# ConvGLU of a hybrid decoder layer: gate, up and down products in 2x2 blocks, seven block products in place of eight

## The chip, the cores and the metric

The kernel runs on one core of one Trainium2 chip. The metric is the device time of one execution in microseconds (us), the median of several runs. TensorE (PE) multiplies, VectorE (DVE), ScalarE (ACT) and GpSimd (POOL) do the elementwise work, SyncE (SP) issues the transfers between DRAM and SBUF, PEld is the loading of TensorE's weights.

## What is computed

One decoder layer on 2048 tokens of 1024 channels in float32: mixers (sliding-window attention and RWKV-7 side by side, not touched here), the output projection with its residual, the ConvGLU and a final norm.

```python
x = x + concatenate([att, rw], axis=-1) @ w_out
h = rms_norm(x, norm2_g)
u = h @ w_gate                                   # (2048,1024) @ (1024,2816)
c = conv_b + sum(conv_w[j] * pad(u)[:, j:j + T] for j in range(3))
x = x + (silu(c) * (h @ w_up)) @ w_down          # (2048,2816) @ (2816,1024)
return rms_norm(x, final_g)
```

## The kernel before

**Precision.** Every operand of the large products is split in a high part (a copy rounded to the matmul type, made on ACT) and a low part (the value minus the high part, on DVE or POOL). `mm3` (L189; through the helper `mm` all matmuls carry L104) adds three matmuls for each 128 rows of the contraction: high x high, high x low, low x high. Each is 128x128 weights against 512 columns.

**Phase A**, until about 1299 us, is the mixers. Its instructions follow an order that is written out by hand. From `order["on"] = False` on (L1236) the Tile framework's scheduler sets the order in which each engine's queue is filled; the queues themselves run in order.

**Output projection, second part.** `o_job` (L1295) makes 128 tokens x 512 output channels with 24 matmuls from the mixers' output (`catT` in DRAM), adds the residual and leaves the row `x2` in `acc` or in DRAM (`x2d`). `half_prep` (L1312) norms four such rows, transposes them (L1328), scales them on ACT and keeps the transposed, split `h` of a half of the tokens (1024) in SBUF: `hh`, `hl`.

**Gate and up.** For each half `hf` and each of 22 tiles `f` of 128 features, `gate_up(f)` loads 512 KB of each weight, splits it (`split_w`, L1269; low part on POOL, L1276) and for two quarters `q` of 512 tokens runs 24 matmuls into `pg` and 24 into `pu`. ACT and DVE apply the convolution over tokens (`cc`; `halo` carries the last two tokens), the silu and the product; `ah` and `al` (POOL, L1385) are the split result, which stays in SBUF.

**Down.** After each two feature tiles `down` (L1388) adds their product with w_down to the rows `acc`: for 8 token tiles and 2 column halves 6 matmuls into `pd` and one addition on DVE. `gate_up` runs one group ahead of `down`. After the last group each row of the half is squared on ACT (`jo`), scaled on DVE with `rso` and `fgb` (the final norm's weights) and written.

The second half's `half_prep` stands between the last `gate_up` and the last two `down` of the first half, so there TensorE always has down matmuls in its queue. PSUM's eight banks are two pools of four: `ps_gu` and `ps_dn`.

Of the kernel before, what the change touches and what calls it, by code (L numbers as in the profile page):

```python
# [83 lines left out]
def hybrid_trunk_kernel(  # L84
# [1152 lines left out]
    # ================= output projection, second part, and ConvGLU =================  # L1237
    with ExitStack() as B:
        h2 = B.enter_context(tc.tile_pool(name="h2", bufs=1))
        sp = B.enter_context(tc.tile_pool(name="fsp", bufs=2))  # L1240
# [13 lines left out]
        fgb = bc.tile([P, D], F32, name="fgb")  # L1254

        def ffn_consts():
# [6 lines left out]
            nc.sync.dma_start(out=fgb, in_=final_g.rearrange("(o d) -> o d", o=1).broadcast_to([P, D]))

        halo = bc.tile([P, NF, 2], F32, name="halo")
        wg3 = ffn_w_gate[0].rearrange("(k p) f -> p k f", p=P)
        wu3 = ffn_w_up[0].rearrange("(k p) f -> p k f", p=P)

        def split_w(src, tag, name, bufs, pool=gp, lpool=None):  # L1269
            s = wp.tile([P, D], F32, tag="st", name=f"s_{name}", bufs=3)  # L1270
            sv = s.rearrange("p (k f) -> p k f", k=NK) if len(src.shape) == 3 else s
            nc.sync.dma_start(out=sv, in_=src)
            a = pool.tile([P, D], F32R, tag=tag + "h", name=f"h_{name}", bufs=bufs)
            l = (lpool or pool).tile([P, D], F32R, tag=tag + "l", name=f"l_{name}", bufs=bufs)
            act(a, s, AF.Copy)
            (tt if tag == "cat" else nc.gpsimd.tensor_tensor)(out=l, in0=s, in1=f32(a), op=ALU.subtract)  # L1276
            return a, l
# [177 lines left out]
```

## Time and profile before

| | |
|---|---|
| median of 3 runs | 2877.03 us (2875.14 to 2879.46) |
| profiled execution, span of its instructions | 2880.8 us |
| TensorE busy | 2814.0 us, 98% |
| DVE, ACT, POOL busy | 49%, 38%, 34% |
| DRAM read, written | 177.35 MB, 27.39 MB |

The span is one execution under the profiler, from its first to its last instruction; it lies 3.8 us above the median of the runs. A busy engine is one with an instruction in it; matmuls overlap each other, so a matmul's own length (390 ns) is more than the distance from one to the next. "Idle before" and "releaser" say what ended an engine's wait.

### The profile page before, as it was taken

Reading aid. Unit: us, or ns where it says so; the run is one execution under the profiler, and the core shown is the slowest. Engines: PE = TensorE matmul, PEld = TensorE weight load, DVE = VectorE, ACT = ScalarE, POOL = GpSimd, SP = SyncE. Lnnn points to the kernel's source line nnn. Section 1 sums busy time; section 2 is a strip of 40 time slices with the busy share of each in tenths; the row PEclk is TensorE's granted clock in tenths of the full one; section 3 lists DMA queues with packets and bytes.
Section 4 is the critical chain, followed back from the end, with each engine's and each line's share of the span. In section 5 each row is a group of like instructions: output and inputs, shape, how many; then the busy total and the mean of one; then the engine's idle time right before and its main releaser. Section 6 shows DMA issues by size and latency. Waiting matters only on the chain.

```text
span 2880.8 us, 41403 instructions
## 1 busy us (share of the span) xinstructions
PE 2814.0 (98%) x16003; PEld 2196.6 (76%) x16003; DVE 1404.7 (49%) x3223; ACT 1108.6 (38%) x2430; POOL 985.1 (34%) x893
## 2 busy tenths in 40 slices
PE   7899999999999999999999999999999999999998
PEld 5567777777767677768788888888888888888887
DVE  5567666766776667435323333333372333333335
ACT  4356555655565556443322222222242222212222
POOL 6334443443434334321143322233333333322232
PEclk8899999999999999999999999999999999999999
DMA  4222222222232222346521111111133111111111
GB/s 123 61 65 66 71 70 67 63 70 71 64 91 61 61 61 73 94 129 198 186 64 47 51 52 45 44 50 53 59 111 109 48 55 47 49 52 44 44 52 59
DMA packets 319159, 207.44 MB, mean 72 GB/s; under 512 B 96704, under 2 KB 285266, under 8 KB 318962
## 3 DMA queue, kind: packets, MB, share of 16 engines
q1 hardware_dynamic: 318354, 204.26, 24.3%
q8 instruction: 126, 2.06, 0.3%
q14 instruction: 71, 0.58, 0.1%
q10 hardware_dynamic: 608, 0.53, 0.1%
HBM read 177.35 MB, written 27.39 MB: 71 GB/s over the span
## 4 chain that ended last, share of the span: by engine, by line
PE 84%; DVE 8%; DMA 4%; ACT 2%; issue 1%; POOL 0%; SPq 0%; ACTq 0%; DVEq 0%; POOLq 0%
PE pg L104 17%; PE pu L104 17%; PE pd L104 16%; PE pc L104 5%; PE po L104 3%; PE pin_r L104 3%; PE pin_k L104 3%; PE pin_q L104 2%; PE poa L104 2%; DVE M L124 2%; PE px L104 2%; DVE Mt L124 2%; PE pS L104 2%; DMA LL<-dL 1%; PE pO L104 1%; PE pin_v L104 1%
## 5 line engine op out<-in xcount | busy, mean ns | idle before, releaser
L124 DVE TENSOR_TENSOR acc<-pd,acc 128x512 f32<-128x512 f32 x352 | 242.6, 691 | 270.1 <-PE pd L104 269.8
L124 DVE SCALAR_TENSOR_TENSOR cc<-pg,fcst,cc 128x511 f32<-128x511 f32 (+1 forms) x176 | 131.9, 749 | 458.9 <-ACT cc L110 455.8
L1385 POOL TENSOR_TENSOR al<-cc,ah 128x512 fp32r<-128x512 f32 x88 | 113.6, 1291 | 477.9 <-ACT ah L110 477.9
L104 PE MATMUL pg<-h2h,l_g 128*128 128x512 f32 x704 | 277.0, 393 | 0.0
L104 PE MATMUL pu<-h2h,l_u 128*128 128x512 f32 x704 | 276.7, 393 | 0.0
L104 PE MATMUL pg<-h2h,h_g 128*128 128x512 f32 x704 | 276.0, 392 | 0.0
L104 PE MATMUL pu<-h2h,h_u 128*128 128x512 f32 x704 | 275.6, 392 | 0.0
L104 PE MATMUL pg<-h2l,h_g 128*128 128x512 f32 x704 | 275.3, 391 | 0.0
L104 PE MATMUL pd<-h_d,ah 128*128 128x512 f32 x704 | 275.1, 391 | 0.0
L104 PE MATMUL pd<-l_d,ah 128*128 128x512 f32 x704 | 275.0, 391 | 0.0
L104 PE MATMUL pd<-h_d,al 128*128 128x512 f32 x704 | 274.7, 390 | 0.0
L104 PE MATMUL pu<-h2l,h_u 128*128 128x512 f32 x704 | 274.6, 390 | 0.0
L110 ACT ACTIVATE cc<-pg,fcst 128x512 f32<-128x512 f32 x88 | 67.8, 770 | 319.6 <-PE pg L104 319.6
L1276 POOL TENSOR_TENSOR l_g<-s_g,h_g 128x1024 fp32r<-128x1024 f32 x44 | 106.2, 2414 | 197.0 <-ACT h_g L110 197.0
L124 DVE TENSOR_TENSOR Mt<-M,LL 128x60 f32<-128x60 f32 (+24 forms) x496 | 154.3, 311 | 35.6 <-DMA LL<-dL 27.0
L1276 POOL TENSOR_TENSOR l_d<-s_d,h_d 128x1024 fp32r<-128x1024 f32 x44 | 105.6, 2401 | 189.6 <-ACT h_d L110 189.6
L124 DVE TENSOR_TENSOR M<-M,Mt 128x60 f32<-128x60 f32 (+24 forms) x496 | 163.7, 330 | 10.9
L124 DVE TENSOR_TENSOR cc<-pu,cc 128x512 f32<-128x512 f32 x88 | 60.9, 692 | 206.4 <-PE pu L104 201.3
L104 PEld LDWEIGHTS pg<-h2l,h_g 128*128 128x128 f32 x704 | 132.2, 188 | 30.2
L104 PEld LDWEIGHTS pu<-h2l,h_u 128*128 128x128 f32 x704 | 132.2, 188 | 30.1
L104 PEld LDWEIGHTS pg<-h2h,l_g 128*128 128x128 f32 x704 | 132.3, 188 | 29.1
L104 PEld LDWEIGHTS pu<-h2h,l_u 128*128 128x128 f32 x704 | 132.3, 188 | 28.8
(324 smaller groups left out, 6407.4 us busy)
## 6 DMA issues: line engine op xcount, KB each, us to landing
s_g<-in_ffn_w_gate_dram SPq DMA_DIRECT2D x44, 512.0 KB
s_u<-in_ffn_w_up_dram SPq DMA_DIRECT2D x44, 512.0 KB
s_d<-in_ffn_w_down_dram SPq DMA_DIRECT2D x44, 512.0 KB
s_cat<-catT SPq DMA_DIRECT2D x20, 512.0 KB
x<-in_x_dram SPq DMA_DIRECT2D x16, 512.0 KB
w_k<-in_w_in_dram SPq DMA_DIRECT2D x16, 512.0 KB
w_r<-in_w_in_dram SPq DMA_DIRECT2D x16, 512.0 KB
w_v<-in_w_in_dram SPq DMA_DIRECT2D x16, 512.0 KB
```

The costliest lines, as they stand in the source:

```text
L104: in_order("pe", nc.tensor.matmul(**kw))
L110: in_order("act", nc.scalar.activation(*args, **kw))
L124: in_order("dve", f(*args, **kw))
L1276: (tt if tag == "cat" else nc.gpsimd.tensor_tensor)(out=l, in0=s, in1=f32(a), op=ALU.subtract)
L1385: nc.gpsimd.tensor_tensor(out=al[:, qs], in0=cc, in1=f32(ah[:, qs]), op=ALU.subtract)
```

## The change

The Strassen-Winograd scheme multiplies two matrices cut in 2x2 blocks with seven block products in place of eight; the blocks are added and subtracted before and after. It is applied twice.

**Gate and up.** A quad is two feature tiles x two quarters of 512 tokens x the contraction in two halves of 4 x 128 rows. It is 7 products of 12 matmuls. `quad_units` makes the seven block sums of the weights on DVE and splits each in `uh` (ACT) and `ul` (POOL, `gsub`, L1255), in a ring of six units. The seven block sums of `h` are made once for each half (`h2_first`, `h2_second`, `h2_third`: 28 splits of 128x512, high on ACT, low on POOL). `quad` runs the products in the order 1, 6, 7, 5, 2, 4, 3; products 2, 4 and 3 are added in the banks of 1, 7 and 5; `take` evacuates. The convolution works on 1024 tokens at a time. For half 1 the 16 raw tiles of `h` are parked in DRAM (`h1raw`) and read when half 0's gate and up are done.

**Down** comes after all of gate and up, for both halves at once: 7 products of 11 steps of 24 matmuls over all eight banks. The seven block sums of the activations are made on DVE (`sa`) when a pair of feature tiles is done and written to DRAM (`actc`), 256 KB for each sum, pair and half; each step of down reads 512 KB of them back and splits them on ACT and POOL. The 22 tiles of w_down (`wd`, 512 KB each) and `fgb` are loaded into memory that gate and up have used; products 1 and 2 load their weights apart (`sb`). The residual rows are read again (`xr`, 32 x 256 KB) and added on POOL after products 2 and 4. The last product's rows are finished after its evacuation.

The pools of the output projection lie over other tiles of phase A than before, and the constants' transpose (`pfc`) is called before the first `o_job`.

```diff
-        ps_gu = B.enter_context(tc.tile_pool(name="ps_gu", bufs=4, space=PSUM))
-        ps_dn = B.enter_context(tc.tile_pool(name="ps_dn", bufs=4, space=PSUM))
+        ps_b = B.enter_context(tc.tile_pool(name="ps_b", bufs=8, space=PSUM, reuse_waits="tile"))
...
+        def h2_split(hf, p, kk, src):
...
+            act(hi, src, AF.Copy)
+            gsub(lo, src, f32(hi))
+            H2[hf, p, kk] = (hi, lo)
...
+        def h2_second(hf, kk, b11, b12, b22):
+            t3 = hp2.tile([P, 512], F32, tag="ht", name=f"t3_{hf}_{kk}", bufs=3)
+            tt(out=t3, in0=b22, in1=b12, op=ALU.subtract)
+            h2_split(hf, 7, kk, t3)
...
+        def quad_units(w3, pr, name):
+            st = quad_load(w3, pr, name)
+            a11, a21 = st[0][:, :, 0:P], st[0][:, :, P:2 * P]
+            a12, a22 = st[1][:, :, 0:P], st[1][:, :, P:2 * P]
+            yield unit(a11, f"{name}_1", shape=4)
+            s3 = up_.tile([P, 512], F32, tag="s3", name=f"s3_{name}", bufs=2).rearrange("p (k f) -> p k f", k=4)
+            vsub(s3, a11, a21)
+            vadd(a21, a21, a22)
+            vsub(a11, a21, a11)
+            yield unit(a11, f"{name}_6", shape=4)
+            yield unit(s3, f"{name}_7", shape=4)
+            yield unit(a21, f"{name}_5", shape=4)
+            vsub(a11, a12, a11)
+            yield unit(a12, f"{name}_2", shape=4)
+            yield unit(a22, f"{name}_4", shape=4)
+            yield unit(a11, f"{name}_3", shape=4)
...
+                if p == 1:
+                    u2 = gp.tile([P, 512], F32, tag="u2", name=f"u2_{name}", bufs=2)
+                    act(u2, ps[1], AF.Copy)
+                elif p == 6:
+                    vadd(u2, ps[6], u2)
+                elif p == 7:
+                    u3 = gp.tile([P, 512], F32, tag="u3", name=f"u3_{name}", bufs=1)
+                    vadd(u3, ps[7], u2)
+                elif p == 5:
+                    take(22, ps[5], u3)
...
+                    act(cc, gr[i][:, 2:], AF.Identity, scale=cw[:, 2, f:f + 1], bias=cb[:, f:f + 1])
+                    stt(out=cc, in0=gr[i][:, 1:HALF + 1], scalar=cw[:, 1, f:f + 1], in1=cc, op0=ALU.mult, op1=ALU.add)
+                    stt(out=cc, in0=gr[i][:, 0:HALF], scalar=cw[:, 0, f:f + 1], in1=cc, op0=ALU.mult, op1=ALU.add)
+                    act(cc, cc, AF.Silu)
...
+                        tmp = gp.tile([P, 512], F32, tag="ct", name=f"ct_{name}_{what}", bufs=2)
+                        vadd(tmp, ps, u)
+                        nc.gpsimd.tensor_tensor(out=cc, in0=tmp, in1=cc, op=ALU.mult)
...
+                vadd(sa[0], c0[:, t2], c1[:, t2])
+                vsub(sa[1], sa[0], c0[:, t1])
+                vsub(c0[:, t2], c0[:, t1], c0[:, t2])
+                vsub(sa[2], c1[:, t1], sa[1])
+                put(5, sa[0])
...
+        wd = [dp.tile([P, D], F32, name=f"wd_{f}") for f in range(NF)]
+        for f in range(NF):
+            nc.sync.dma_start(out=wd[f], in_=ffn_w_down[0, f * P:(f + 1) * P, :])
...
+        for p in ORDER:
+            if p in (1, 6, 7, 5):
+                banks = [bank(f"d{p}_{m}") for m in range(8)]
+            for k in range(NPR):
+                ahead(NU_)
+                ah0, ah1, bu = ready.pop(0), ready.pop(0), ready.pop(0)
+                for m in range(8):
+                    a = (ah0, ah1)[m // 4]
+                    ms_ = slice((m % 4) * P, (m % 4 + 1) * P)
+                    mm3(banks[m], [(a[0][:, ms_], a[1][:, ms_], bu[0], bu[1])],
+                        first=k == 0 and p in (1, 6, 7, 5), last=k == NPR - 1, skip_group_check=p in (2, 4, 3))
+            for m in range(8):
...
+                elif p == 5:
+                    vadd(u3[m], banks[m], u3[m])
+                    square(u3[m], 1, m, 1)
+                    finish(1, m, c21[m], u3[m])
+                else:
+                    vadd(u2[m], banks[m], u2[m])
+                    square(u2[m], 0, m, 1)
+                    finish(0, m, c11[m], u2[m])
```

Three places in the order of the queues. In the rows the numbers at the end of a name are buffer numbers.

POOL's queue between the halves, before (`l_g`, `l_u`: splits of a whole weight tile; `al`: of activations; `ms_f`, `rs_f`: the norm's factors, one number for each row):

```order
L1276 TENSOR_TENSOR l_u_21_19586<-s_u_21_19583,h_u_21_19585 128x1024
L1385 TENSOR_TENSOR al_20_19454<-cc_20_1_19566,ah_20_19453 128x512
L1385 TENSOR_TENSOR al_21_19590<-cc_21_0_19641,ah_21_19589 128x512
L1276 TENSOR_TENSOR l_g_0_20308<-s_g_0_20305,h_g_0_20307 128x1024
L132 TENSOR_SCALAR ms_f_19732<-ms_f_19732 128x1
L132 TENSOR_TENSOR rs_f_19734<-ms_f_19732,mhalf 128x1
L132 TENSOR_SCALAR ms_f_19741<-ms_f_19741 128x1
L132 TENSOR_TENSOR rs_f_19743<-ms_f_19741,mhalf 128x1
```

and now (`h2l_p_kk`: low parts of block sum p of h; `ul`: of weights):

```order
L1255 TENSOR_TENSOR ul_g_0_1_19126<-s_g_0_0_19121,uh_g_0_1_19125 128x512
L1255 TENSOR_TENSOR h2l_7_0_19269<-t_1_0_19266,h2h_7_0_19268 128x512
L1255 TENSOR_TENSOR h2l_7_1_19289<-t_1_1_19286,h2h_7_1_19288 128x512
L1255 TENSOR_TENSOR h2l_7_2_19309<-t_1_2_19306,h2h_7_2_19308 128x512
L1255 TENSOR_TENSOR h2l_5_0_19279<-hr_0_1_19262,h2h_5_0_19278 128x512
L1255 TENSOR_TENSOR h2l_5_1_19299<-hr_1_1_19282,h2h_5_1_19298 128x512
L1255 TENSOR_TENSOR h2l_5_2_19319<-hr_2_1_19302,h2h_5_2_19318 128x512
L1255 TENSOR_TENSOR ul_g_0_6_19149<-s_g_0_0_19121,uh_g_0_6_19148 128x512
L1570 TENSOR_TENSOR cc_21_19055<-ct_u_10_22_19165,cc_21_19055 128x512
L1255 TENSOR_TENSOR ul_g_0_7_19169<-s_g_0_19144,uh_g_0_7_19168 128x512
```

Where small rows stood, 28 splits of h stand among the splits of the next quads' weights.

SP's queue at the end of gate and up: before, the loads of a group's weights stand one after the other to the end:

```order
L1272 DMA s_g_21_24400<-in_ffn_w_gate_dram 128x8x128
L1272 DMA s_u_21_24406<-in_ffn_w_up_dram 128x8x128
L1272 DMA s_d_18_24535<-in_ffn_w_down_dram 128x1024
L1272 DMA s_d_19_24541<-in_ffn_w_down_dram 128x1024
L1272 DMA s_d_20_24675<-in_ffn_w_down_dram 128x1024
L1272 DMA s_d_21_24681<-in_ffn_w_down_dram 128x1024
```

Now (`sa_k`, `sb_k`: activations and weights of step k of product 1, counted from 0):

```order
L1466 DMA sb_3_22925<-in_ffn_w_down_dram 128x512
L1577 DMA actc_10_15831<-sa_1_10_22707 128x512
L1577 DMA actc_10_15809<-sa_1_10_22708 128x512
L1577 DMA actc_10_15820<-cc_20_22565 128x512
L1577 DMA actc_10_15864<-sa_1_10_22709 128x512
L1611 DMA fgb<-in_final_g_dram 128x1024
L1614 DMA wd_22729<-in_ffn_w_down_dram 128x1024
L1614 DMA wd_22730<-in_ffn_w_down_dram 128x1024
...
L1614 DMA wd_22750<-in_ffn_w_down_dram 128x1024
L1466 DMA sb_4_22965<-in_ffn_w_down_dram 128x512
L1461 DMA sa_5_22995<-actc_5_15793 128x1024
```

The last sums of the activations are written, then come `fgb` and all 22 tiles of w_down, then the fifth step's weights.

DVE's queue at the end of the program, before (`acc<-pd`: additions, the others the final scaling):

```order
L124 TENSOR_TENSOR acc_6_20295<-pd_20_6_0_24783,acc_6_20295 128x512
L124 TENSOR_TENSOR acc_6_20295<-pd_20_6_1_24791,acc_6_20295 128x512
L124 TENSOR_TENSOR acc_7_20296<-pd_20_7_0_24799,acc_7_20296 128x512
L124 SCALAR_TENSOR_TENSOR acc_5_20294<-acc_5_20294,rso_24880,fgb 128x512 x2
L124 TENSOR_TENSOR acc_7_20296<-pd_20_7_1_24807,acc_7_20296 128x512
L124 SCALAR_TENSOR_TENSOR acc_6_20295<-acc_6_20295,rso_24892,fgb 128x512 x2
L124 SCALAR_TENSOR_TENSOR acc_7_20296<-acc_7_20296,rso_24904,fgb 128x512 x2
```

and now (`cu`: evacuations of the last product's banks `d`; `c_`: the rows' other half):

```order
L1429 TENSOR_TENSOR cu_3_22784<-d_3_25188,cu_3_22784 128x512
L1429 TENSOR_TENSOR cu_4_22785<-d_4_25189,cu_4_22785 128x512
L124 SCALAR_TENSOR_TENSOR c_0_22773<-c_0_22773,rso_26108,fgb 128x512
L124 SCALAR_TENSOR_TENSOR cu_0_22781<-cu_0_22781,rso_26108,fgb 128x512
L1429 TENSOR_TENSOR cu_5_22786<-d_5_25190,cu_5_22786 128x512
L124 SCALAR_TENSOR_TENSOR c_1_22774<-c_1_22774,rso_26118,fgb 128x512
L124 SCALAR_TENSOR_TENSOR cu_1_22782<-cu_1_22782,rso_26118,fgb 128x512
L1429 TENSOR_TENSOR cu_6_22787<-d_6_25191,cu_6_22787 128x512
L1429 TENSOR_TENSOR cu_7_22788<-d_7_25192,cu_7_22788 128x512
L124 SCALAR_TENSOR_TENSOR c_2_22775<-c_2_22775,rso_26128,fgb 128x512
```

Before, a row is complete every 2.7 us or so of matmuls and is scaled between them; now all eight rows of the last product are complete within its last step, and 16 scalings follow their 8 evacuations.

## Rows read from the trace of the kernel before

**Rows 1.** The page, its first two parts: span; TensorE's busy time, the engines; the span in 40 slices for PE, the granted clock and the DMA.

```profile
span 2880.8 us, 41403 instructions
PE 2814.0 (98%) x16003; PEld 2196.6 (76%) x16003; DVE 1404.7 (49%) x3223; ACT 1108.6 (38%) x2430; POOL 985.1 (34%) x893
PE   7899999999999999999999999999999999999998
PEclk8899999999999999999999999999999999999999
DMA  4222222222232222346521111111133111111111
```

**Rows 2.** The page's chain of the work that ended last: shares of the span by engine, and by line.

```profile
PE 84%; DVE 8%; DMA 4%; ACT 2%; issue 1%; POOL 0%; SPq 0%; ACTq 0%; DVEq 0%; POOLq 0%
PE pg L104 17%; PE pu L104 17%; PE pd L104 16%; PE pc L104 5%; PE po L104 3%; PE pin_r L104 3%; PE pin_k L104 3%; PE pin_q L104 2%; PE poa L104 2%; DVE M L124 2%; PE px L104 2%; DVE Mt L124 2%; PE pS L104 2%; DMA LL<-dL 1%; PE pO L104 1%; P
```

**Rows 3.** The same chain in order of time, in gate and up of half 0: start, length, what.

```profile
1603.57 5.49 PE pg L104 x24
1609.06 5.49 PE pu L104 x24
```

**Rows 4.** Groups of instructions from 1285 us on, three of the nine groups of ConvGLU's matmuls: count, busy time and mean ns of one, idle time before them.

```profile
L104 PE MATMUL pg<-h2h,l_g 128*128 128x512 f32 x704 | 277.0, 393 | 0.0
L104 PE MATMUL pu<-h2h,h_u 128*128 128x512 f32 x704 | 275.6, 392 | 0.0
L104 PE MATMUL pd<-h_d,ah 128*128 128x512 f32 x704 | 275.1, 391 | 0.0
```

**Rows 5.** Stretches of the span: length, then busy time (and instructions) of PE, PEld, DVE, ACT, POOL, granted clock, DMA share, GB/s. Before the output projection's second part, in it, in gate/up/down of half 0 and half 1, and the end.

```profile
1285.00:1300.00 15.00, 13.31 (x57) 10.36 (x57) 9.26 (x12) 5.07 (x8) 4.33 (x3) 1.00 0.79 247
1320.00:1416.00 96.00, 93.22 (x435) 76.71 (x434) 46.47 (x59) 34.97 (x48) 9.39 (x11) 0.98 0.63 197
1500.00:2000.00 500.00, 500.00 (x2189) 410.69 (x2188) 165.85 (x277) 109.24 (x166) 147.57 (x75) 1.00 0.16 49
2300.00:2800.00 500.00, 500.00 (x2188) 410.72 (x2187) 165.71 (x277) 109.69 (x152) 153.29 (x78) 1.00 0.17 50
2860.00:2881.00 21.00, 12.86 (x57) 10.33 (x55) 15.74 (x24) 7.52 (x22) 7.45 (x13) 0.88 0.47 176
```

**Rows 6.** Timeline of PE in the mixers' last gap: the first po matmul and the last one before the mixers go on.

```profile
1282.71 0.50 PE L104 MATMUL po<-woh,h_cat 128*128 128x512 f32 x1 [0.39 <-ACT woh L110]
1289.90 0.40 PE L104 MATMUL po<-woh,h_cat 128*128 128x512 f32 x1
```

**Rows 7.** Timeline in half 0: issue of one 512 KB load, and the copy that waited for it.

```profile
1464.29 0.34 SPq L1272 DMA_DIRECT2D s_d<-in_ffn_w_down_dram  x1
1467.96 1.06 ACT L110 ACTIVATE h_d<-s_d 128x1024 fp32r<-128x1024 f32 x1 [0.74 <-DMA s_d<-in_ffn_w_down_dram]
```

**Rows 8.** Groups of instructions from 1285 us on, on POOL, DVE and ACT: busy time, mean ns of one, idle time before.

```profile
L1385 POOL TENSOR_TENSOR al<-cc,ah 128x512 fp32r<-128x512 f32 x88 | 113.6, 1291 | 477.9 <-ACT ah L110 477.9
L110 ACT ACTIVATE cc<-pg,fcst 128x512 f32<-128x512 f32 x88 | 67.8, 770 | 319.6 <-PE pg L104 319.6
L124 DVE TENSOR_TENSOR l_cat<-s_cat,h_cat 128x1024 fp32r<-128x1024 f32 x19 | 23.3, 1224 | 5.5 <-ACT h_cat L110 5.4
L124 DVE SCALAR_TENSOR_TENSOR acc<-acc,rso,fgb 128x512 f32<-128x512 f32 x32 | 22.4, 745 | 2.6 <-POOL rso L132 2.6
L110 ACT ACTIVATE h2h<-pt,fcst 128x512 fp32r<-128x512 f32 x32 | 20.0, 683 | 21.8 <-PE pt L1328 21.6
L132 POOL TENSOR_TENSOR rs_f<-ms_f,mhalf 128x1 f32<-128x1 f32 x16 | 9.8, 614 | 1.2
L1323 DVE TENSOR_SCALAR xn<-acc,rs_f 128x1024 f32<-128x1024 f32 x8 | 6.0, 753 | 5.2 <-POOL rs_f L132 5.1
L132 POOL TENSOR_SCALAR ms_f<-ms_f 128x1 f32<-128x1 f32 x16 | 6.0, 375 | 75.5 <-ACT xn L110 55.8 <-ACT sq L110 19.7
```

**Rows 9.** Three tiles and DVE's instructions on them: count, then shortest, median and longest in ns, first and last start. hl is a split in the mixers, wol one in the output projection.

```profile
L124 DVE TENSOR_TENSOR hl<-hr,hh x24: 683/693/1770, 262.3 to 1149.0; 128x512 fp32r<-128x512 f32 x24
L124 DVE TENSOR_TENSOR wol<-swo,woh x16: 677/685/1775, 1283.3 to 1396.2; 128x512 fp32r<-128x512 f32 x16
L124 DVE TENSOR_TENSOR acc<-pd,acc x352: 674/692/693, 1484.7 to 2873.5; 128x512 f32<-128x512 f32 x176
```

**Rows 10.** Stretches as in rows 5 where the transfers are dense: in the output projection, and where half 1's rows are read.

```profile
1308.00:1312.00 4.00, 4.00 (x20) 3.30 (x19) 2.35 (x4) 1.39 (x3) 0.81 (x2) 1.00 1.02 349
1312.00:1316.00 4.00, 4.00 (x19) 3.34 (x18) 2.61 (x3) 1.86 (x3) 0.79 (x2) 1.00 1.08 370
2122.00:2126.00 4.00, 4.00 (x19) 3.33 (x18) 2.49 (x4) 2.30 (x4) 1.76 (x4) 1.00 0.91 357
```

**Rows 11.** Timeline of PE where matmuls of 512 columns follow the mixers' small ones.

```profile
1272.82 0.31 PE L104 MATMUL pO<-ptl,vth 128*64 128x128 f32 x1
1274.00 0.63 PE L104 MATMUL poa<-hh,wl_c 128*128 128x512 f32 x1
1274.42 0.63 PE L104 MATMUL poa<-hh,wh_c 128*128 128x512 f32 x1
```

**Rows 12.** Timeline at the end: the last matmul and the last scaling (two).

```profile
2872.47 0.39 PE L104 MATMUL pd<-h_d,al 128*128 128x512 f32 x1
2876.34 1.41 DVE L124 SCALAR_TENSOR_TENSOR acc<-acc,rso,fgb 128x512 f32<-128x512 f32 x2 [0.85 <-POOL rso L132]
```

More of the change, by code (lines that the diff above doesn't have):

```diff
@@ L1259, in ffn_consts @@
             nc.sync.dma_start(out=frow[8 + NF:], in_=conv_w[0].rearrange("i (j p) -> (i j) p", p=P))
-            ps = ps_gu.tile([P, 512], F32, tag="gu", name="pfc")[:, :8 + 4 * NF]
+            ps = bank("pfc")[:, :8 + 4 * NF]
             nc.tensor.transpose(out=ps, in_=frow, identity=ident[:8 + 4 * NF, :8 + 4 * NF])
             nc.vector.tensor_copy(out=fcst, in_=ps)
[L1263 to L1277, printed above, removed]
         def wo_half(e):
@@ new lines, in product, with quad @@
+        def product(ps, u, hf, p, first, last):
+            mm3(ps, [(u[0][:, kk * P:(kk + 1) * P], u[1][:, kk * P:(kk + 1) * P], *H2[hf, p, kk]) for kk in range(4)],
+                first=first, last=last, skip_group_check=not first)
+        def quad(hf, name, take):
+            ps = {}
+            for p in PRODS:
+                ahead(NU_)
+                u = ready.pop(0)
+                if p in (1, 6, 7, 5):
+                    ps[p] = bank(f"q{p}_{name}")
+                    product(ps[p], u, hf, p, True, True)
+                else:
+                    b = {2: 1, 4: 7, 3: 5}[p]
+                    product(ps[b], u, hf, p, False, True)
+                if p == 1:
[8 more added lines that the diff above has]
+                    take(22, ps[5], u3)
+                elif p == 2:
+                    take(11, ps[1], None)
+                elif p == 4:
+                    take(21, ps[7], u2)
+                else:
+                    take(12, ps[5], u2)
@@ new lines, in hybrid_trunk_kernel, with all_units, ahead @@
+        ORDER = (1, 2, 6, 7, 4, 5, 3)
+        steps = [(p, k) for p in ORDER for k in range(NPR)]
+        jobs = [(hf, pr, g) for hf in range(NHALF) for pr in range(NPR) for g in (True, False)]
+        ready = []
+        def all_units():
+            for hf, pr, g in jobs:
+                yield from quad_units(wg3 if g else wu3, pr, f"{'g' if g else 'u'}{hf}_{pr}")
+            for p, k in steps:
+                yield from down_units(p, k)
+        source = all_units()
+        def ahead(n):
+            while len(ready) < n:
+                u = next(source, None)
+                if u is None:
+                    return
+                ready.append(u)
@@ new lines, in finish @@
+        def finish(j, m, ca, cb_):
+            i = tok[j][m]
+            ms = MS[i]
+            rs = sp_.tile([P, 1], F32, tag="rso", name=f"rso_{i}", bufs=4)
+            gts(out=rs, in0=ms[0], scalar1=ms[1], scalar2=RMS_EPS, op0=ALU.add, op1=ALU.add)
+            gtt(out=rs, in0=rs, in1=mhalf[:, 0:1], op=ALU.pow)
+            for e, c in enumerate((ca, cb_)):
+                es = slice(512 * e, 512 * e + 512)
+                stt(out=c, in0=c, scalar=rs, in1=fgb[:, es], op0=ALU.mult, op1=ALU.mult)
+                nc.sync.dma_start(out=out_t[i][:, es], in_=c)
```

358 lines of the change are left out of this document (236 added, 122 removed).

## The prediction, as it was made

> **What bounds the kernel now.** I read the page first. TensorE is busy for 98% of the span at the full granted clock, the other engines for half of it or less, and the DMA for a fifth or less outside one peak [rows 1]. The chain of the work that ended last is TensorE for 84%, and its largest entries are ConvGLU's products pg, pu and pd [rows 2]. In ConvGLU the chain runs through whole groups of 24 matmuls with no other engine between them, 5.49 us a group, so 5.49 / 24 = 0.2288 us a matmul [rows 3]. The nine groups of these matmuls, 704 each, have one length [rows 4]: 9 x 704 = 6336. By stage, TensorE has no idle time in the middle of either half; 2.78 us of it lie in the output projection's stage, 1.69 just before, 8.14 in the last 21 us [rows 5]. So before, a matmul more or less in ConvGLU is 0.2288 us, and nothing else there has a price. The question is whether this stays so when the other engines get more work.
>
> **What it removes.** The changed order has 3696 matmuls for gate/up and 1848 for down, of the same shape (128x128 against 512 columns): 5544, so 792 fewer. 792 x 0.2288 = **181.2 us** less, if TensorE is as seldom idle. What follows are the stalls.
>
> **(a) Output projection and start of gate/up: 18 us.** Before, pieces of the output projection fill the mixers' last gap, 1282.7 to 1290.1: 20 matmuls, 4.6 us [rows 6]. Now its tiles lie over tiles that the last poa reads, so it starts after it: +4.6. The transpose pfc now stands ahead of the first po; its three small loads are queued on SP behind the last x2d write. A 512 KB load takes 3.67 us from issue to use [rows 7]; I take 4 (0 to 6). The weights of the second half of po's contraction come later too: 3. Transposes stand right behind the fourth, eighth and last po group and need the normed rows: after adding and squaring, ms_f 0.375, rs_f 0.614, the scaling 0.753 [rows 8], partly under 24 matmuls of the next group: 3 in all. Gate/up starts after eight copies of 0.683 and one POOL split of 1.291 [rows 8], 6.8 less the transposes meanwhile: 6.5. Sum 21.1, less the 2.8 us of the old stage's own idle time: 18 (bounds 5 and 30).
>
> **(b) Steady gate/up: 12 us.** One pair of feature tiles is 168 matmuls, 38.4 us. In it POOL has 14 splits of 128x512 and 3 products, 17 x 1.291 = 21.9 [rows 8], and 4 small copies: 23.1 (at 0.3 us each, an estimate). DVE has 12 sums of 128x512 from SBUF at 0.69, 4 scalar_tensor_tensor of 128x1024 at about 1.28 (an estimate between 1.224 for that width and 2 x 0.745, [rows 8]) and 11 evacuations from PSUM at 0.69: 21. Each alone fits, at 60% and 55%. But the rows of the same operation show two lengths: hl takes 693 ns in the median and 1770 at most, wol 685 and 1775, while acc<-pd, whose one input is in PSUM, stays between 674 and 693 in 352 times [rows 9]. A DVE instruction with both inputs in SBUF waits for a POOL instruction that runs. So what the two have to do one after the other is 23.1 + 12 x 0.69 + 4 x 1.28 = 36.5 us of 38.4: it fits by 1.9 us. If instead each of the 16 is pushed back by 1.08 us (1.77 - 0.69), DVE needs 21 + 17.3 = 38.3: as long as TensorE. The weight splits are made up to 6 products ahead (16 us), which smooths this; the third sum u3 has only some 2 us before the product that reuses its bank. I take 0.55 us a pair, 22 pairs: **12** (0 to 60).
>
> The Trainium skill (SBUF — State Buffer, Who interferes with whom) says that a VectorE instruction with two SBUF inputs and a GpSimd instruction that reads SBUF exclude each other, whoever issues first holds the port, and the other blocks fully; one with a PSUM input is free. The rows of hl, wol and acc<-pd agree. By that rule the forecast holds only while each of the two always has other work ready when the port is taken; where they also wait for each other's data, the pair goes the way of the first two rivals below.
>
> **(c) Between the halves: 20 us.** The first rewrite of h for half 1 must wait for the last quad's first product; from there POOL's queue holds 41 operations of 1.291 us up to the split ul that product 6 of half 1's first "up" quad needs (28 of them splits of h, in rows as the order shows): 52.9 us, begun 1.9 us late (the copy and the wait for the quad's first matmuls). TensorE has some 160 matmuls, 36.6 us, ahead of that use in its own order: 52.9 + 1.9 - 36.6 = 18.2; with the copy and DVE's sums between them 20 (to 32, if the 20 DVE sums of 0.69 exclude POOL). Before, POOL had small rows and no split of h there.
>
> **(d) From gate/up to down: 23.5 us.** SP's queue has fgb and 22 tiles of w_down, 12.06 MB, ahead of the small weights of the fifth step of product 1, and they may only land in memory that gate/up frees at its end. A full queue moves 349 to 370 GB/s [rows 10]: 34.5 us at 350. They start about 6 us after gate/up's last matmul (the last activations must be summed and written first) and DVE has 32 sums of these tiles in its queue ahead of the fifth split. TensorE has four steps, 4 x 24 x 0.2288 = 22 us. It waits from 22 to about 44: 22, and 1.5 for the clock, which before fell to half for four matmuls (pitch 0.43) after 64- and 128-column work [rows 11]. Bounds 17 (390 GB/s) and 50 (200).
>
> **(e) Between products of down: 4.** Eight evacuations at 0.69 to 0.77 each [rows 8, 9] against 8 banks that are needed 0.69 us apart: seen only at the ends. Product 5 carries 46 POOL operations, 59.4 us of its 60.4. Bounds 0 and 15.
>
> **(f) Tail: 7.5.** Before, 7.9 us lie between the last matmul and the end [rows 12]. Now DVE has 8 evacuations (0.69) and 16 scalings (0.745) after the first bank is final, 17.4 us, of which 4.8 lie beside the last matmuls; with 2.8 for the last write as before: 15.4. So 7.5 (4 to 10).
>
> **Sum** against the profiled span: 2880.8 - 181.2 + 18 + 12 + 20 + 23.5 + 4 + 7.5 = 2784.6. The median of the runs shown, 2877.0, lies 3.8 below that span, so the forecast is **2781 us**. The activations' way through DRAM (77 x 0.52 MB = 40 MB written and 40 read) I cost at nothing outside (d): a step of down reads 0.52 MB in 5.49 us, 95 GB/s against 349 and more [rows 10], and gate/up's DMA share before is 0.16 [rows 5]; without that cover a step would wait the 3.7 us of its load [rows 7].
>
> **Rivals.** First, **POOL and DVE pace gate/up**: DVE pushed back by POOL each time (38.3) plus about 2 us of waiting for TensorE's sums in the same queue gives 40.5 a pair, 2.1 more than TensorE: 22 x 2.1 = 46 in place of 12, **2815 us**. For it: 36.5 of 38.4 on one shared path. Against it: the six-product lookahead.
>
> Second, the other side, **DVE's queue becomes the bound outright**: its sums of SBUF tiles stand in order behind POOL's split and product of the same tile (2 x 1.291) and the scaled copy from ACT, some 6 us a pair on top of 38.3: 44.5, 22 x 6.1 = 134 in place of 12: **2903 us**, slower. It decides from (181.2 - 73) / 22 = 4.9 us of loss a pair, 43.3 us. Against it: these waits must all fall where nothing else is ready, while the scheduler ordered the queue.
>
> Third, **the boundaries are hidden better**: if the queue's transfers start tile by tile while gate/up still runs and POOL's row is interleaved, (c), (d) and (a) halve: losses 45, **2741 us**. Against it: in SP's order the loads stand behind the last write.
>
> That the change does not do what it says is out: the matmuls are counted in its order. DRAM slower at the refill (200 GB/s) adds 26 us and lies within the range.
>
> **How the numbers follow.** Forecast 0.58, first rival 0.26, third 0.08, DVE as bound 0.06, within 0.2% (5.8 us, about what a measurement of this kernel can tell from no change) 0.02. Range 2738 to 2842: from the third case to the first rival with (d) at its upper bound. Faster 0.92, same 0.02, slower 0.06.
>
> **What would show it.** ConvGLU's matmuls still 0.2288 us apart with gaps only at the named places; a pair of tiles in 38.4 to 39.5 us. (a) first q matmul near 1435; (c) one gap of 15 to 30 us early in half 1, released by POOL's ul or h2l; (d) a gap of some 20 us in product 1 of down at its fifth step, with DMA near 350 GB/s; (f) 15 us behind the last matmul. Wrong if pairs take over 40 us with DVE or POOL as releaser, or if the idle time sits elsewhere.

## The result, and the profile after

The changed kernel takes **2812.48 us** (median of 4 runs, 2803.73 to 2816.21) against 2876.14 (4 runs): ratio 0.978, 95% interval 0.976 to 0.980. It is faster, and the time lies within the predicted range, 31 us above the forecast of 2781.

The page of the changed kernel, the lines that answer to [rows 1] and [rows 2]: span, busy times, the span in 40 slices for PE, granted clock and DMA, and the chain's shares by engine.

```profile
span 2812.9 us, 41981 instructions
PE 2672.6 (95%) x15211; PEld 2061.7 (73%) x15211; DVE 1702.4 (61%) x3186; ACT 1291.3 (46%) x2733; POOL 1444.8 (51%) x1355
PE   7899999999999999998889999997999997999997
PEclk8899999999999999999999999998999999999999
DMA  4222222222223222336473233332333336543354
PE 78%; DVE 8%; DMA 4%; POOL 4%; issue 3%; ACT 2%; SPq 0%; ACTq 0%; DVEq 0%; POOLq 0%
```

TensorE has 15211 matmuls, 792 fewer, and is idle in new places: the slices with 8 and 7 in the middle. POOL is now on the chain. Stretches of the changed kernel (columns as in [rows 5]): the output projection, gate and up, between the halves, the start of down, down, and behind the last matmul.

```profile
1360.00:1400.00 40.00, 32.23 (x125) 26.05 (x126) 34.09 (x27) 24.12 (x40) 33.92 (x26) 0.83 0.41 132
1600.00:1700.00 100.00, 100.00 (x432) 81.13 (x431) 66.50 (x68) 37.94 (x55) 68.03 (x56) 1.00 0.32 101
1880.00:1935.00 55.00, 34.80 (x113) 23.43 (x112) 34.28 (x25) 18.41 (x33) 54.96 (x39) 0.77 0.25 82
2372.00:2394.00 22.00, 1.44 (x7) 0.86 (x5) 18.08 (x27) 0.42 (x1) 0.00 (x0) 0.62 1.03 408
2500.00:2700.00 200.00, 200.00 (x884) 165.65 (x883) 71.57 (x70) 72.08 (x130) 120.12 (x91) 1.00 0.38 119
2798.00:2813.00 15.00, 0.00 (x0) 0.00 (x0) 11.18 (x18) 2.06 (x6) 8.20 (x11) 0.58 0.74 280
```

Read the PE column against the length: in gate and up it is full, in 1360 to 1400, in 1880 to 1935 and in 2372 to 2394 it isn't, and there the granted clock (0.83, 0.77, 0.62) falls too. Between the halves POOL is busy 54.96 of 55 us; at the start of down the DMA is full (1.03, 408 GB/s) and DVE is busy 18.08 of 22 us, with the block sums of the w_down tiles as they land. What TensorE waited for (engine, tile it writes and line, then the releaser; us in total, times, longest), the rows of ConvGLU and the output projection:

```profile
PE d L104 <- ACT uh_b L110: 20.8, 1, 20.8
PE q_g L104 <- POOL h2l L1255: 10.1, 5, 3.2
PE po L104 <- DVE catl L124: 7.9, 4, 6.1
PE pt L1328 <- DVE xn L1322: 7.3, 4, 2.3
PE q_u L104 <- POOL ul_u L1255: 5.5, 1, 5.5
PE q_g L104 <- ACT uh_g L110: 4.6, 1, 4.6
PE d L104 <- DVE ul_b L1426: 3.7, 2, 3.3
PE pfc L1281 <- DMA frow<-in_conv_w_dram: 3.5, 1, 3.5
PE po L104 <- ACT cath L110: 3.2, 2, 2.5
PE q_g L104 <- POOL ul_g L1255: 3.0, 1, 3.0
```

Where the 181.2 us went, from the matmuls' start times in the two traces. "Gaps" is what distances over 0.73 us have beyond 0.2288; "slow" is the same of the distances between 0.33 and 0.73 us, that is, matmuls at the lower clock (1.2 GHz) and short waits:

| stretch | longer than its matmuls x 0.2288 us, against before | forecast |
|---|---|---|
| (a) last poa to the first q: 163.3 us. Before 118.0 + 3.7 of po done earlier (16 matmuls) + 6.9 for the 64 transposes that moved here | 34.7 (in it gaps 29.0, slow 8.1; before 3.1 and 1.8) | 18 |
| (b) + (c) gate and up: 892.6 against 3696 x 0.2288 = 845.6 | 47.0: distance between matmuls 15, gaps 23.7, slow 8.6 | 12 + 20 |
| (d) + (e) down: 446.3 against 1848 x 0.2288 = 422.8 | 23.5: gaps 21.0 and 4.0, slow 2.1, shorter distance -3.6 | 23.5 + 4 |
| (f) behind the last matmul: 14.9 against 7.9 | 7.0 | 7.5 |
| mixers, same instructions | 0.3 | 0 |

Sum 112.5: 181.2 - 112.5 = 68.7; the two spans differ by 67.9.

### The profile page after: what moved, and what is told of

It is laid out like the page before. It is cut to its first block, busy times and chain, and to the rows that moved or that the text cites. A ratio compares the mean times of both kernels' runs of the same rounds, so it can differ in the third digit from the quotient of the medians.

```text
span 2812.9 us, 41981 instructions
## 1 busy us (share of the span) xinstructions
PE 2672.6 (95%) x15211; PEld 2061.7 (73%) x15211; DVE 1702.4 (61%) x3186; ACT 1291.3 (46%) x2733; POOL 1444.8 (51%) x1355
## 4 chain that ended last, share of the span: by engine, by line
PE 78%; DVE 8%; DMA 4%; POOL 4%; issue 3%; ACT 2%; SPq 0%; ACTq 0%; DVEq 0%; POOLq 0%
PE q_g L104 15%; PE q_u L104 15%; PE d L104 14%; PE pc L104 6%; PE pin_r L104 3%; PE pin_k L104 3%; PE pin_q L104 3%; POOL h2l L1255 2%; PE poa L104 2%; PE px L104 2%; PE pS L104 2%; DVE M L124 2%; DVE Mt L124 2%; PE pO L104 2%; PE pin_v L104 2%
## 5 line engine op out<-in xcount | busy, mean ns | idle before, releaser
L1255 POOL TENSOR_TENSOR ul_a<-sa,uh_a 128x512 fp32r<-128x512 f32 x154 | 205.7, 1340 | 182.2 <-ACT uh_a L110 182.1
L1255 POOL TENSOR_TENSOR ul_u<-s_u,uh_u 128x512 fp32r<-128x512 f32 x154 | 207.9, 1358 | 165.9 <-ACT uh_u L110 162.8
L104 PE MATMUL q_g<-h2l,uh_g 128*128 128x512 f32 x616 | 246.1, 400 | 10.1 <-POOL h2l L1255 10.1
L1255 POOL TENSOR_TENSOR ul_g<-s_g,uh_g 128x512 fp32r<-128x512 f32 x154 | 211.2, 1376 | 77.5 <-ACT uh_g L110 77.5
L104 PE MATMUL q_g<-h2h,uh_g 128*128 128x512 f32 x616 | 245.3, 398 | 5.2 <-ACT uh_g L110 4.6
L104 PE MATMUL q_u<-h2h,ul_u 128*128 128x512 f32 x616 | 244.4, 397 | 5.5 <-POOL ul_u L1255 5.5
L104 PE MATMUL q_g<-h2h,ul_g 128*128 128x512 f32 x616 | 245.7, 399 | 3.2 <-POOL ul_g L1255 3.0
L104 PE MATMUL q_u<-h2h,uh_u 128*128 128x512 f32 x616 | 244.7, 397 | 0.9 <-DVE ct_u L1429 0.7
L104 PE MATMUL q_u<-h2l,uh_u 128*128 128x512 f32 x616 | 244.3, 397 | 0.0
L104 PE MATMUL d<-ul_b,uh_a 128*128 128x512 f32 x616 | 232.7, 390 | 3.7 <-DVE ul_b L1426 3.7
L104 PE MATMUL d<-uh_b,ul_a 128*128 128x512 f32 x616 | 229.7, 390 | 0.0
L104 PE MATMUL d<-uh_b,uh_a 128*128 128x512 f32 x616 | 206.4, 393 | 20.8 <-ACT uh_b L110 20.8
L104 PEld LDWEIGHTS d<-uh_b,uh_a 128*128 128x128 f32 x616 | 116.7, 190 | 45.5 <-ACT uh_b L110 21.2
```

Source lines behind the costliest of these rows:

```text
L104: in_order("pe", nc.tensor.matmul(**kw))
L1255: nc.gpsimd.tensor_tensor(out=out, in0=in0, in1=in1, op=ALU.subtract)
```

## Experiments

The mixers' end moves from run to run although their instructions don't (the last poa matmul starts between 1282.7 and 1295.4 us in the traces below), so single terms are read from the four stretches of the table, and the whole from the ratio to the kernel before, which ran on the same chip each time. Ratio of the changed kernel: 0.978. The stretches scatter too: in runs whose edit lies elsewhere (a) takes 162.5 to 166.1 us, gate and up 891.7 to 893.8, down 445.9 to 451.8 (counted from its own first matmul, as below), the tail 14.4 to 14.9.

### e1: w_down by steps

```diff
-        for f in range(NF):
-            nc.sync.dma_start(out=wd[f], in_=ffn_w_down[0, f * P:(f + 1) * P, :])
...
                 ahead(NU_)
+                if p in (1, 2):
+                    f = k + NPR * (p - 1)
+                    i = nc.sync.dma_start(out=wd[f], in_=ffn_w_down[0, f * P:(f + 1) * P, :])
+                    tc.add_manual_dep(i.ins, LAST[0].ins.name, ..., reason="issue order")
```

`LAST[0]` is the last load `sb`, so SP issues the tile behind it.

> One tile of w_down is loaded per step of down's products 1 and 2, behind that step's own small weights, instead of all 22 ahead of the fifth step. Theory (the refill in SP's order is the wait between gate/up and down): the 20.98 us gap at down's fifth step goes, to under 4 us, with it the slow clock behind it, and the span falls by 18 to 22 us against the changed kernel (about 2792 us). Rival (the wait is for memory or DMA throughput, whatever the order): the gap is spread over products 1 and 2, in sum still over 12 us.

2786.9 us, ratio 0.969 (0.965 to 0.972). Down takes 425.0 us in place of 446.1, gaps 4.0 in place of 25.0. TensorE's waits from 2340 us on, and the stretch at the start of down:

```profile
PE d L104 <- DVE ul_b L1426: 3.7, 2, 3.3
2345.00:2420.00 75.00, 75.00 (x333) 62.05 (x332) 41.05 (x40) 28.00 (x48) 40.05 (x29) 1.00 0.79 280
```

Theory right: the wait of 20.8 us is gone and TensorE full, while the DMA still moves 280 GB/s. The order on SP was the wait, not the bandwidth.

### e2: low parts of half 1's h on DVE

```diff
-            gsub(lo, src, f32(hi))
+            (tt if hf == 1 else nc.gpsimd.tensor_tensor)(out=lo, in0=src, in1=f32(hi), op=ALU.subtract)
```

> The 28 low parts of half 1's block sums of h are made on DVE, not POOL. Theory (POOL's queue of 41 operations alone sets the gap between the halves): the gaps from 1880 to 1935 us, 23 us in sum, and the half clock there, some 10 us, go to under 5 together, the span falls by 25 to 33 us. Rival (DVE is next: 28 more operations beside 16 sums and the pair's own 21 us, about 51 us against 36.6 of matmuls): 12 to 18 us of gaps stay, now released by DVE, the span falls by 10 to 18 us.

2794.15 us, ratio 0.972 (0.966 to 0.977). Gate and up take 879.6 us in place of 892.6; gaps between the halves 13.8 in place of 23.2, slow 2.7 in place of 7.0. The stretch between the halves and TensorE's largest waits in it:

```profile
1870.00:1925.00 55.00, 42.41 (x168) 31.71 (x167) 50.52 (x59) 25.90 (x46) 29.03 (x18) 0.91 0.30 99
PE q_u L104 <- POOL ul_u L1255: 7.1, 1, 7.1
PE q_g L104 <- DVE h2l L124: 3.0, 4, 1.0
```

The rival's size: POOL's row was most of it, and behind it comes DVE, now busy 50.5 of 55 us. The longest wait that is left, 7.1 us, ends with POOL's `ul_u`, and DVE is behind that as well. The product that stands ahead of it in POOL's queue takes 5.85 us in place of 1.29, while DVE runs eight operations with two SBUF inputs one right behind the other, from 1905.04 to 1909.94 us. POOL's product, and the stretch of these operations:

```profile
1905.20 5.85 POOL L1570 TENSOR_TENSOR cc<-ct_u,cc 128x512 f32<-128x512 f32 x1 [4.24 <-DVE ct_u L1429]
1905.00:1910.00 5.00, 0.28 (x2) 0.00 (x0) 4.93 (x9) 0.63 (x1) 4.80 (x1) 0.53 0.00 0
```

### e3: low parts of half 0's h on DVE

The same line with `hf == 0`.

> The 28 low parts of half 0's block sums of h, made during the output projection, are made on DVE, not POOL. Theory (DVE's and POOL's operations on SBUF exclude each other there, DVE 34.1 us busy in 1360 to 1400 with 27 operations): although DVE gets 19 us more work, its operations return to 0.69 and 1.22 us, the 10.8 us of gaps from 1357 to 1394 and the half clock behind them (6.8 us) shrink by more than half, and the span falls by 8 to 18 us. Rival (DVE is simply short of time there): gaps of the same size or larger, span the same or up to 10 us more.

2793.32 us, ratio 0.972 (0.968 to 0.976). The stretch (a) takes 152.0 us in place of 163.3. The split `catl` on DVE (shortest, median, longest in ns), first in the changed kernel:

```profile
L124 DVE TENSOR_TENSOR catl<-s_cat,cath x20: 1214/1226/2322, 1296.4 to 1440.1; 128x1024 fp32r<-128x1024 f32 x20
```

then in this run, with the stretch that answers to 1360 to 1400:

```profile
L124 DVE TENSOR_TENSOR catl<-s_cat,cath x20: 1211/1218/1226, 1285.1 to 1417.7; 128x1024 fp32r<-128x1024 f32 x20
1350.00:1390.00 40.00, 39.53 (x175) 32.33 (x175) 35.57 (x53) 26.21 (x42) 11.85 (x8) 1.00 0.54 176
```

DVE has 53 instructions in 35.57 us where it had 27 in 34.09. With POOL's splits gone no catl is pushed back, and TensorE is full at the full clock. Of its waits in the stretch (a), those for catl were 7.9 us and those for xn 7.3; here they are:

```profile
PE pt L1328 <- DVE xn L1322: 5.3, 3, 2.1
PE po L104 <- DVE catl L124: 1.1, 2, 0.5
```

Theory right: DVE was not short of time, it stood behind POOL.

### e4: the constants' transpose after the first po

```diff
-        ffn_consts()
         nc.vector.memset(halo, 0.0)
...
+            if i == 0:
+                ffn_consts()
             if i == 3:
```

> The constants' transpose is called after the first output projection job, not before it. Theory (it holds up the whole stage): the 3.68 us gap before pfc goes, with half of the slow clock in 1300 to 1320 (2.6 us), span lower by 3 to 6 us. Rival (the split of the first rows of the mixers' output, landed at 1308.5 us, is the next wait): under 2 us are gained.

2817.79 us, ratio 0.979 (0.975 to 0.983): nothing gained, the stretch (a) is 171.7 us, 8.4 longer. Of the chain in order of time (start, length, what):

```profile
1305.57 0.70 DVE xt L124
...
1306.29 0.33 SPq L1313
...
1307.40 3.98 DMA frow<-in_conv_w_dram
...
1311.52 0.39 PE pfc L1281
```

Both theories missed it. The call was moved, and with it its three loads, in SP's queue behind the write of the first x2 row (L1313), which waits for the first po to be added: a gap of 6.3 us before pfc in place of 3.7. Other gaps before the first po matmuls (4.6 and 2.5 us, for weights and for a split) come up as well. The loads would have to be issued earlier, not the transpose later; no run tried this.

### e5 and e11: more work on POOL

```diff
             lo(l_, src, f32(h_))
+            if shape is not None and name[0] == "u":
+                j_ = up_.tile([P, 512], F32, tag="jk", name=f"jk_{name}", bufs=1).rearrange(...)
+                gsub(j_, src, f32(h_))          # e5;  e11: gsub(j_, f32(h_), f32(h_))
```

> Every weight split of the up quads is done twice on POOL (the second result is not used): 7 more operations of 1.29 us for each pair of feature tiles. POOL then has 32 us of its own in a pair, still less than TensorE's 39. Theory of the shared path (a POOL operation and a DVE operation with two SBUF inputs run one after the other, 36.5 us a pair before, 45.5 now): the pair takes 44 to 47 us, gate/up 120 to 170 us longer than 892.6. Rival (each engine's own sum counts, contention is hidden by the six products of lead): the pair stays at 39 to 40 us, gate/up less than 25 us longer, most of it between the halves.

2922.41 us (one run). The steady pairs take 41.3 to 47.2 us, 44.4 in the mean, gate and up 1003.7 us, 111 longer. But not by the shared path alone. One wait of DVE in 1500 to 1850 us:

```profile
DVE s_u L1429 <- POOL jk_u L1255: 22.3, 8, 2.8
```

DVE's sums in place had to wait until the added operation had read its source, a chain that the expectation had left out. So the second run:

> As the run with added POOL work, but the 7 more operations for each pair read the unit's high part alone (subtracted from itself, result not used), so DVE's next block sum in place no longer waits for them; only the unit's buffer is held longer. Theory (the shared path): the pair again takes 43 to 46 us, gate/up 90 to 130 us longer than 892.6. Rival (in the earlier run DVE waited for the data that the added operations read, 59 us in sum): the pair stays under 41 us, gate/up less than 45 us longer.

2859.05 us (one run). Steady pairs take 39.9 to 43.0 us, 41.3 in the mean, gate and up 944.3 us, 51.7 longer. Stretch 1500 to 1850 us:

```profile
1500.00:1850.00 350.00, 338.46 (x1434) 269.54 (x1433) 230.24 (x231) 121.45 (x179) 293.88 (x237) 1.00 0.30 97
```

Between the two: POOL is busy 84% of the time, TensorE still 97%. The added operations read one tile and are shorter than the expectation took them to be, 1.045 us in the median in place of 1.29:

```profile
L1255 POOL TENSOR_TENSOR jk_u<-uh_u x154: 1031/1045/2095, 1465.1 to 2388.0; 128x512 f32<-128x512 f32 x154
PE q_u L104 <- DVE u_u L1432: 10.9, 8, 1.8
DVE s_g L1432 <- DMA s_g<-in_ffn_w_gate_dram: 35.6, 8, 5.3
```

So what excludes each other adds up to 36.5 + 7 x 1.045 = 43.8 us, not 45.5, and the pair takes 2.5 less than that. The margin is small, as forecast: seven short operations in a pair cost 2.2 us. That the exclusion alone costs them isn't shown. TensorE waits for DVE's evacuation `u_u`, and DVE, whose queue runs in order, had before it waited 35.6 us for loads of gate weights (2.9 in the changed kernel in the same 350 us), whose buffers come free only after POOL's splits. In one pair a POOL split ends at 1609.2 us, the load that waited for it lands at 1613.0, and TensorE goes on at 1616.4. Between e5 and e11 the loss falls from 111 to 52 us, but the added operations also became shorter, so how much of e5's loss was the wait for data stays open.

### e6: high and low tiles apart

```diff
+        h2b = G.enter_context(tc.tile_pool(name="h2b", bufs=1, side="right", reuse_waits="tile"))
...
-            lo = h2.tile([P, 512], F32R, tag=f"l{p}{kk}", ...)
+            lo = h2b.tile([P, 512], F32R, tag=f"l{p}{kk}", ...)
```

> The high and low tiles of h's block sums lie in two pools (57 KB apart) in place of next to each other (2 KB apart); the instructions stay. Theory (the longer distance between gate/up's matmuls, 0.2329 us against 0.2287 before and 0.2267 in down, comes from where their moving operands lie): it falls to 0.227 to 0.230, 10 to 20 us less. Rival (the place is not it): 0.2325 to 0.2333, no change of the span over 4 us.

2807.72 us (one run). Gate and up 892.5 us, distance 0.2329 us: nothing moved. That theory is out.

### e7: the tail on ACT

```diff
                     square(c11[m], 0, m, 0)
+                    tt(out=c11[m], in0=c11[m], in1=fgb[:, 0:512], op=ALU.mult)
...
-                stt(out=c, in0=c, scalar=rs, in1=fgb[:, es], op0=ALU.mult, op1=ALU.mult)
+                if e == 0:
+                    act(c, c, AF.Copy, scale=rs)
+                else:
+                    stt(out=c, in0=c, scalar=rs, in1=fgb[:, es], op0=ALU.mult, op1=ALU.mult)
```

(and the same multiplication for c21).

> The first column half of every row is multiplied by the final norm's weights after products 2 and 4 (16 more multiplications on DVE, off the end) and scaled by the row's factor on ACT at the end; DVE's queue at the end falls from 8 x 0.69 + 16 x 0.745 to 8 x 0.69 + 8 x 0.745. Theory (DVE's queue is the tail and the 3.5 us gap at product 3's start): the 14.9 us behind the last matmul fall to 8 to 10, the gap of 3.48 us near 2750 to under 1.5, span 6 to 9 us less. Rival (the row factors, ACT's squares and POOL, take over): 12 us or more stay behind the last matmul.

2813.52 us, ratio 0.978 (0.975 to 0.981): nothing gained. Behind the last matmul 12.5 us in place of 14.9, and the chain there is now POOL's row factors:

```profile
2799.04 0.86 POOL rso L132 x2
...
2801.10 1.18 POOL rso L132 x2
```

The rival's case. And the 16 multiplications weren't free where they were put: gaps in down 30.1 in place of 25.0 and slow 5.9 in place of 2.1, down 9.0 us longer (up to 5.7 of that also appear in runs that leave down alone). TensorE there waits 3.0 us in five times for POOL's `ul_a`, and never in the changed kernel. What was saved at the end, 2.4 us, came back earlier.

### e8 and e9: together

e8 is e1, e3, e7 and, of e2, the products 1, 7, 6 and 5 (2, 4 and 3 stay on POOL).

> Together: one tile of w_down per step, low parts of half 0's h sums on DVE, of half 1's products 1, 7, 6, 5 on DVE and 2, 4, 3 on POOL, the tail on ACT. If the waits lie at different places they add: 21 (down), 11 (output projection), 13 to 20 (between the halves), 6 to 9 (tail), 51 to 61 us less than the changed kernel, 2752 to 2762 us, ratio to the kernel before 0.956 to 0.961. Rival (a saved wait comes back later at the next engine): under 40 us.

2765.45 us, ratio 0.962 (0.959 to 0.965). By stretches: (a) 12.3 less, gate and up 6.7, down 16.7, tail 2.5: 38.2, the rival's size (the span fell by 50.8, but 12.7 of that are the mixers). Sharing half 1's splits was worse than all on DVE (885.9 us against e2's 879.6). Down takes 4.4 us more than in e1, with the tail's multiplications in it; in e9, without them, 1.3 more, so some 3 us may be theirs, which is within the scatter.

e9 is e1 with all low parts of h on DVE, in both halves, and the tail as it was.

> One tile of w_down per step, and all low parts of h's block sums on DVE in both halves; the tail as in the changed kernel. The three savings lie at different places and were measured apart: 21.1 us in down, 11.3 in the output projection, 13.0 between the halves. If they add: the three stretches are 45 us shorter in sum, ratio to the kernel before 0.960 to 0.964. Rival (they share a cause or push a wait on): under 35 us.

2763.16 us (6 runs), ratio 0.962 (0.960 to 0.964): it beats both kernels. (a) 152.8 us, gate and up 881.1, down 426.3: 10.5 + 11.5 + 19.8 = 41.8 us less in sum, of 45 expected. The first line of its page:

```profile
span 2766.5 us, 41951 instructions
```

The three waits lie at different places and have causes of their own.

### e10: without the weights' sums and splits

```diff
             act(h_, src, AF.Copy)
+            if shape is not None:
+                return hi, hi
             lo(l_, src, f32(h_))
...
-            vsub(s3, a11, a21)
-            vadd(a21, a21, a22)
-            vsub(a11, a21, a11)
...
-            vsub(a11, a12, a11)
```

> Left out in gate and up: the block sums of the weights (DVE) and the low parts of the weights (POOL; the high part is multiplied in their place). TensorE has the same matmuls, POOL 14 operations of 1.29 us and DVE 8 sums less in each pair. Theory (the distance of 0.2329 us between matmuls there, against 0.2267 in down, comes from the work of POOL and DVE beside them): it falls to 0.227 to 0.230. Rival (it belongs to TensorE's own instruction stream): it stays at 0.232 to 0.234. In both cases the gaps between the halves shrink, since POOL's queue there loses 10 of 41 operations: from 23 to 8 to 14 us.

2792.0 us (one run). Gate and up 873.4 us, gaps between the halves 9.7. A stretch in steady gate and up:

```profile
1600.00:1700.00 100.00, 100.00 (x432) 81.09 (x431) 37.74 (x49) 34.94 (x51) 15.13 (x18) 1.00 0.33 108
```

POOL's 68 us have become 15, DVE's 66.5 have become 38, and TensorE starts the same 432 matmuls in 100 us. The longer distance is not the work of POOL and DVE beside it. The shorter gap between the halves agrees with POOL's row as its cause.

## Why the prediction was right or wrong

**Right: the direction, the removed matmuls, and the ends of the sum.** The matmul count is as forecast. (d): a gap of 20.98 us at the fifth step, forecast 22; e1 shows the cause by removing it. The chain there ends in three pieces of one load queue:

```profile
2361.76 10.56 DMA wd<-in_ffn_w_down_dram
2372.34 10.22 DMA wd<-in_ffn_w_down_dram
2382.58 10.22 DMA wd<-in_ffn_w_down_dram
```

From the issue of `fgb` at 2358.4 us to the last landing at 2392.8 the refill took 34.4 us; from 350 GB/s I had worked out 34.5. The slow matmuls behind the gap at the lower clock are 1.6, forecast 1.5. (e): 4.0, forecast 4. That (d) and (e) together came out 4 us under the forecast is mostly the shorter distance between down's matmuls, 0.2267 us, which no term has. (f): 14.9 us behind the last matmul, forecast 15.4.

**Near in size by luck, with the wrong mechanism: (b).** 12 us forecast, 15 measured. I had put it on waits of TensorE for POOL and DVE; there are none in steady gate and up. What is longer is the distance between matmuls, 0.2329 us in place of 0.2288. The chain of a pair of feature tiles (168 matmuls) is TensorE alone, 24 matmuls in 5.57 us where [rows 3] have 5.49:

```profile
1617.44 13.72 PE q_g L104 x59
1631.16 0.23 PE q_u L104
1631.39 5.57 PE q_g L104 x24
```

Every steady pair takes 39.04 us in half 0 and 39.20 in half 1, to the hundredth. The forecast's mechanism is wrong here, and the first rival's too: the time of 2812 is near its 2815, but no pair is paced by POOL or DVE. The contention itself is as the rows said:

```profile
L124 DVE SCALAR_TENSOR_TENSOR cc<-g,fcst,cc x88: 1271/1794/2348, 1482.7 to 2336.3; 128x1024 f32<-128x1024 f32 x88
L1429 DVE TENSOR_TENSOR sa<-cc,cc x22: 693/1765/1771, 1504.9 to 2354.2; 128x512 f32<-128x512 f32 x22
L1429 DVE TENSOR_TENSOR g<-q_g,u_g x66: 675/684/693, 1476.5 to 2332.5; 128x512 f32<-128x512 f32 x66
```

These two operations with two SBUF inputs take 1.79 in place of 1.27 and 1.77 in place of 0.69 us in the median, the one from PSUM never more than 0.693. The Trainium skill (SBUF — State Buffer, Summary: rules for kernel authors) says that the second to issue blocks fully until the first is done. The trace agrees, operation by operation; a POOL split, and a DVE sum that starts just behind it:

```profile
1620.52 1.29 POOL L1255 TENSOR_TENSOR ul_g<-s_g,uh_g 128x512 fp32r<-128x512 f32 x1
1620.59 1.76 DVE L1429 TENSOR_TENSOR sa<-cc,cc 128x512 f32<-128x512 f32 x1 [2.35 <-POOL cc L1570]
```

Of the 108 sums of this size with both inputs in SBUF in 1500 to 1850 us, 46 start while POOL runs, and all 46 end 0.545 to 0.554 us after POOL's operation does; alone they take 0.68. So successive operations overlap by some 0.13 us, which a sum of lengths doesn't count. POOL or one of these DVE operations runs during 33.6 us of a pair of 39.04, where the prediction had 36.5 of 38.4 (its 0.3 us for a small copy is in no row; the shortest takes 0.18). In e11 it is 39.4 of 41.3. That the lead of six products hides what contention there is, is argued; no run changed the lead.

**Wrong: (a), 35 in place of 18.** The step that failed is its list of waits. It priced the later weights (3), pfc (4), the transposes (3) and the start of gate and up (6.5); TensorE's waits for them are 0.5, 3.5, 8.4 (`pt`, with one of 1.1 for xt) and 4.6. It has no term for the splits of the mixers' output, `catl` and `cath`, 11.1 us. Behind both stand the 28 splits of half 0's h that POOL gets in that stage: the prediction gave them no price there, nor what they do to DVE, although (b) had read from [rows 9] that a DVE split stands behind a POOL operation. 11.3 us go with these splits (e3), most of it the waits for catl. The 5.4 us that then still lie above the forecast were not taken apart; in e3's stretch the transposes wait 7.4 us, and 4.1 us are matmuls at the lower clock, which the prediction priced in (d) only. The first term was also miscounted: in the mixers' last gap there are 16 matmuls of po, 3.7 us, not 20.

**Mis-sized: (c), 30 in place of 20.** The mechanism was right: POOL's row (54.96 of 55 us busy), most gaps released by h2l, ul_g and ul_u, and shorter when operations leave it (e2, e10). The gaps between the halves are 23.2 us, 3.2 more than forecast, and six of over 1 us in place of one. The other 7.0 are slow, 6.1 of them matmuls at the lower clock (granted 0.77 there), which had no price in (c). POOL's operations also got longer than the 1.291 of [rows 8], since the exclusion works both ways:

```profile
L1255 POOL TENSOR_TENSOR h2l<-hr,h2h x40: 1251/1528/2291, 1336.4 to 1933.2; 128x512 fp32r<-128x512 f32 x40
```

Against the profiled span the forecast was 28.3 us short (2784.6 and 2812.9): 17 in (a), 10 in (c), 2 behind (a) in the first quads of gate and up, 3 in (b), less 4 in (d) and (e) together. By the clock granted at each matmul's start, 13.8 us are matmuls at the lower clock in (a) and in gate and up (6.2 and 7.6), of which 1.4 were there before. The other 3 us up to the 31 of the medians are the step from span to median: 3.8 us before, 0.4 now.

**The other rivals.** DVE as the bound: not near, DVE is busy 67% in gate and up. Hidden boundaries: no (and with (a), (c) and (d) halved the losses add up to 54 us and the time to 2750, not to 45 and 2741); but e9 shows that it takes three small edits to hide nearly all of (d), a third of (a) and a third of (c).

## What to carry to other kernels

When a change takes work from the busiest engine, price the stages where buffers are refilled, operation by operation and with the other engine's operations that stand behind each: there a helper's queue has no lead, while in the steady part, with six units of lead, none of the helper's delays reached TensorE. Add the slower clock to every group of short gaps; here it was a fifth to a quarter of the gaps again (6.2 us with 29.0, 6.1 with 23.2), and 1.6 behind the one gap of 21 us. Before a call is moved, look at which loads it brings along and behind which write they will queue.

## What the runs showed of the hardware that was not expected

- **The distance between equal matmuls differs by stage, at a granted clock of 1.00.** 128x128 on 512 columns: 0.2267 us in down, 0.2329 in gate and up of the changed kernel (0.2324 in half 0, 0.2333 in half 1), in a pattern that repeats every seven matmuls (230, 233, 240, 232, 232, 232, 227 ns); about 0.229 to 0.230 in gate and up before. It is not the place of the high and low tiles (e6) and not DVE's and POOL's work (e10). What it is stays open; it is worth 15 us here.
- **POOL and DVE wait for each other in full, and DVE can keep POOL out.** DVE's split of 128x1024 goes from 1.22 to 2.32 us, POOL's of 128x512 from 1.29 to as much as 2.29. Where DVE has eight operations with two SBUF inputs one right behind the other, POOL's product waits for all of them, 5.85 us in place of 1.29 (e2). In e9, the fastest kernel, TensorE's longest wait between the halves still ends with the POOL split behind that product, 6.6 us.
- **A full load queue moved 408 GB/s** from DRAM to SBUF in 2372 to 2394 us, more than the 349 to 370 of [rows 10], with TensorE, ACT and POOL all but idle and DVE busy for 18.08 of the 22 us.
